# First stage of a hybrid Hyena / FNet / mLSTM block: sums of squares by matmul, one pass for norm and modulation, other load order, two projection blocks accumulated feature by feature

## The chip, the cores and the metric

The kernel runs on one core of a Trainium2 chip. The metric is the device time of one execution in microseconds (us). The engines are called PE (TensorE, with PEld for its weight loads), DVE (VectorE), ACT (ScalarE), POOL (GpSimd) and SP (SyncE, which here only issues DMAs).

## What is computed

One layer over 1024 latent tokens and 256 context tokens of 1024 features. Only the head of it matters here:

```python
mod_l = jnp.split((jax.nn.silu(c) @ ada_w[l] + ada_b[l])[:, None, :], 6, axis=-1)
mod_c = jnp.split((jax.nn.silu(c_ctx) @ ada_w[l] + ada_b[l])[None, None, :], 6, axis=-1)
zc = modulate(rmsnorm(ctx, norm1_w[l]), mod_c[0], mod_c[1]) @ w_in[l] + b_in[l]
zl = modulate(rmsnorm(x, norm1_w[l]), mod_l[0], mod_l[1]) @ w_in[l] + b_in[l]
```

with `rmsnorm(x, w) = x * rsqrt(mean(x*x) + 1e-6) * w` and `modulate(h, shift, scale) = h * (1 + scale) + shift`. Behind it come the three branches, their gated sum, and a mixture of experts.

## The kernel before

Tokens are held transposed: `xs[k]`, k from 0 to 7, is a tile of 128 features by 1024 tokens. PE gets its precision by splitting: a float32 tile becomes `hi` (rounded to fp32r by a copy on ACT) and `lo` (the rest, by a subtraction on DVE; `split`, L213), and `mm3` (L228) issues three fp32r matmuls, hi by hi, hi by lo, lo by hi (L230 to L232). A plain float32 matmul is two MATMUL records in the trace; an fp32r one is one.

`stage_start` (L283) issues the loads on SP's queue in this order: eight of `xs` (512 KB each), the modulation's weights `aw[0..15]` (512 KB each, L321, in `RB` = 6 buffers of tag "r", so the seventh waits until the first is used up), among them the first projection block's weights. Then `ada_first` (L323) runs:

- `norm_in` (L425): eight squares on ACT (L431), added up by seven additions on DVE (L433); eight float32 matmuls with one column (L439) sum over the 128 partitions; square root on ACT (L441, with eps as bias), reciprocal on DVE (L442); a diagonal matrix (L444) and two float32 matmuls (L448) spread r over the partitions into PSUM; eight multiplications on DVE scale `xs` in place (L450).
- four groups g, each for features 2g and 2g+1: eight k-slices of `silu(c) @ ada_w` (L344) into four rows (some in fp32r pieces split beforehand, the others in float32), a copy to SBUF (L347), four small transposes (L350), small additions and a multiplication for shift and scale (L353 to L357), then per feature a `modulate` pass on DVE (L367) and a `split`.

After `ada_first` come `filt_mlp` (L492; two small matmul layers, L501, with a sine between), `ctx_in`, `filt_fold`, and `stage_proj` (L735), whose first loop projects four blocks of `w_fn` (L745): each is 2 halves x 8 features x 3 = 48 matmuls of L230 to L232 into `gp`, followed by blocks of `w_gate`. Tile's scheduler sets the order of each engine's instructions from a list by priority, so work of these functions is interleaved; each engine then runs its list strictly in order.

Of the kernel before, what the change touches and what calls it, by code (L numbers as in the profile page):

```python
# [16 lines left out]
D = 1024  # L17
L = 1024
# [5 lines left out]
EPS = 1e-6  # L24
# [140 lines left out]
class Prog:  # L165
# [22 lines left out]
        self.n += 1  # L188
        return self.dp.tile(list(shape), dt, name=f"{name}_{self.n}", tag=f"{name}_{self.n}")

    PSB = {"gp": 2, "q": 4, "pb": 1, "acc": 6, "ph": 8}

    def ps(self, tag="pb", shape=(128, 1024)):
        self.n += 1
        pool = self.pg if tag == "gp" else self.pp
        return pool.tile(list(shape), F32, name=f"{tag}_{self.n}", tag=tag, bufs=self.PSB[tag])

    def psum(self, name):
# [84 lines left out]
    def stage_start(self):  # L283
        nc = self.nc
        self.pool("T")
        self.pool("TC", "right")
        self.pool("P")
        self.pool("F1", "right")

        self.cs = self.const([128, 8, 4], F32, "cs")  # L290
        nc.gpsimd.memset(self.cs, 0.0)
        cs = self.cs[:, :, 0:2]
        nc.scalar.activation(cs, self.cvec, AF.Silu)
        self.csr = self.const([128, 8, 4], F32R, "csr")
        self.split(self.csr[:, :, 0:2], self.csr[:, :, 2:4], cs)

        nc.scalar.activation(self.const([128, 1], F32, "se"), self.eps, AF.Sqrt)
        self.modc = self.const([128, 48], F32, "modc")
        self.filt_loads()
        self.norm_load()  # L300
        self.ada_loads(0, 12)
        self.w0 = self.load("P", "w", 3, self.A["w_fn"][0], (128, 8, 128))
        self.ada_loads(12, 16)
        self.filt_loads3(0)
        nc.sync.dma_start(self.skip, self.A["skip"])
        self.ada_first()
        self.filt_mlp()
        self.psum("proj")
        self.ctx_in()
        self.filt_fold()  # L310
        self.close("F1")
        self.pool("F2", "right")
        self.filt_spectra()
        self.close("F2")
# [8 lines left out]
    def ada_first(self):  # L323

        nc = self.nc
        ab = self.const([128, 4, 4], F32, "ab")
        for g in range(4):
            nc.vector.tensor_copy(ab[:, g, 0:2], self.ada_b[:, 2 * g:2 * g + 2])
            nc.vector.tensor_scalar(ab[:, g, 2:4], self.ada_b[:, 8 + 2 * g:10 + 2 * g], 1.0, None, op0=ALU.add)
        self.sc, self.sh = self.const([128, 8, 2], F32, "sc"), self.const([128, 8, 2], F32, "sh")  # L330
        self.norm_in()
        self.hT = {"l": []}
        for g in range(4):

            p = self.ps("q", (128, 512))[:4]
            for i in range(4):
                w = self.aw[4 * g + i]
                two = g < 2 and i % 2 == 0
                ws = self.parts("P", "w", 2, w) if two else (w,)
                for j in range(2):  # L340
                    kk = 2 * i + j
                    for x in ws:
                        c = self.csr if two else self.cs
                        nc.tensor.matmul(p, c[:, kk, :], x[:, 512 * j:512 * j + 512], start=kk == 0 and x is ws[0],  # L344
                                         stop=kk == 7)
            row = self.t("F1", "ft", 8, F32, (4, 512))
            nc.scalar.copy(row, p)  # L347
            q = self.ps("q", (128, 4, 4))
            for i in range(4):
                nc.tensor.transpose(q[:, i, :], row[:, 128 * i:128 * i + 128], self.ident[:4, :4])  # L350
            ks = 2 * g, 2 * g + 1
            m = self.t("TC", "m", 2, F32, (128, 4, 2))
            nc.vector.tensor_add(m, q[:, :, 0:2], ab[:, g, :].unsqueeze(2).to_broadcast([128, 4, 2]))  # L353
            nc.vector.tensor_add(m, m, q[:, :, 2:4])
            nc.vector.tensor_copy(self.sh[:, 2 * g:2 * g + 2, :], m[:, 0:2, :])

            nc.vector.tensor_mul(self.sc[:, 2 * g:2 * g + 2, :], m[:, 2:4, :],  # L357
                                 self.n1[:, 2 * g:2 * g + 2].unsqueeze(2).to_broadcast([128, 2, 2]))
            for k in ks:
                t = self.xs[k]  # L360
                self.modulate(t, k, 0)
                hi, lo = self.t("T", "ht", 18, F32R), self.t("T", "ht", 18, F32R)
                self.split(hi, lo, t)
                self.hT["l"].append((hi, lo))

    def modulate(self, t, k, ci):
        self.nc.vector.tensor_scalar(t, t, self.sc[:, k, ci:ci + 1], self.sh[:, k, ci:ci + 1], op0=ALU.mult, op1=ALU.add)  # L367
# [54 lines left out]
    def norm_load(self):  # L422
        self.xs = [self.load("T", "ht", 18, self.A["x_t"][k]) for k in range(8)]

    def norm_in(self):  # L425

        nc = self.nc
        xs = self.xs
        for k in range(8):
            s = self.t("F1", "ft", 8)  # L430
            nc.scalar.activation(s, xs[k], AF.Square)  # L431
            if k:
                nc.vector.tensor_add(acc, acc, s)  # L433
            else:
                acc = s

        p = self.ps("q", (128, 8))
        for t in range(8):
            nc.tensor.matmul(p[:, t:t + 1], acc[:, 128 * t:128 * t + 128], self.ones[:, :1], start=True, stop=True)  # L439
        r = self.const([128, 8], F32, "r")  # L440
        nc.scalar.activation(r, p, AF.Sqrt, bias=self.eps, scale=1.0 / D)  # L441
        nc.vector.reciprocal(r, r)  # L442
        dg = self.t("F1", "ft", 8)
        nc.vector.tensor_mul(dg.rearrange("p (t c) -> p t c", t=8), self.ident.unsqueeze(1).to_broadcast([128, 8, 128]),  # L444
                             r.unsqueeze(2).to_broadcast([128, 8, 128]))
        p = self.ps("pb")
        for a in (0, 512):
            nc.tensor.matmul(p[:, a:a + 512], self.ones, dg[:, a:a + 512], start=True, stop=True)  # L448
        for k in range(8):
            nc.vector.tensor_mul(xs[k], xs[k], p)  # L450


    def filt_loads(self):
# [281 lines left out]
    def stage_proj(self):  # L735
        nc = self.nc
        A = self.A
        bc = self.b_cols
# [2 lines left out]
        self.pool("U")  # L741
        self.yd = self.dram([3, 4, 128, L], name="yd")

        self.fzd = self.dram([4, 128, L], name="fzd")
        for m in range(4):  # L745
            z = self.t("P", "z", 2)
            w = self.wblock(A["w_fn"][m]) if m else self.parts("P", "w", 2, self.w0)
            self.proj_t(w, self.bias_to(z, bc[:, 12 + m:13 + m]))
            nc.sync.dma_start(self.fzd[m], z)

        self.gd = self.dram([3, 8, 128, L], name="gd")
# [14 lines left out]
        for which, n in (("l", L), ("c", LC)):  # L766
            g = self.dram([2, 36, n], name="g" + which)
# [58 lines left out]
        for m in range(8):  # L826
            if m > 1:
                next(tokens)
            w = self.wblock(A["w_qk"][m])
            z = self.t("P", "z", 2)  # L830
# [9 lines left out]
            if m >= 4:  # L840
                z = self.t("U", "zc", 1, F32, (128, LC))
# [12 lines left out]
        for m in range(12):  # L854
            z = self.t("P", "z", 2)
# [1288 lines left out]
```

## Time and profile before

| | |
|---|---|
| three runs, median (lowest to highest) | 1710.73 us (1708.02 to 1713.69) |
| the profiled execution | 1704.3 us |
| its span, first to last instruction | 1702.6 us |
| PE busy in the span | 1572.0 us (92%) |
| DVE busy | 1193.5 us (70%) |
| ACT busy | 679.9 us (40%) |
| POOL busy | 326.4 us (19%) |

The page of the profile gives busy times; the timeline gives each instruction's start and length in us; the windows view gives, for a stretch, each engine's busy time, the granted TensorE clock (PEclk, 1.00 is 2.4 GHz, 0.50 is 1.2 GHz) and the DMA traffic. PEclk comes from records of changes: before the first record it reads 1.00 whatever the clock was.

### The profile page before, as it was taken

What the parts mean: (1) busy time and instruction counts of PE and PEld (TensorE: products, weight loads), DVE (VectorE), ACT (ScalarE), POOL (GpSimd) and SP (SyncE); (2) the same over time, 40 slices, a digit from 0 to 9 for tenths busy, and PEclk for the clock granted to TensorE, in tenths of its full rate; (3) what the DMA queues carried; (4) which work ended last, traced back from release to release, by engine and by line L of the source; (5) the groups of instructions that cost most, each with busy time, mean ns of one, the idle gap of its engine ahead of it and who ended that gap; (6) DMA issues with size and microseconds to landing.
All of it is one profiled execution on the core that took longest, in us unless ns stands there. A gap on an engine that the chain in (4) does not pass through costs nothing. (4 is left out here: it accounts for less than half of the span.)

```text
span 1702.6 us, 22672 instructions
## 1 busy us (share of the span) xinstructions
PE 1572.0 (92%) x8473; PEld 1297.5 (76%) x8473; DVE 1193.5 (70%) x1831; ACT 679.9 (40%) x1029; POOL 326.4 (19%) x288
## 2 busy tenths in 40 slices
PE   3999999999999999899989888899999969999992
PEld 1477777788888887778877777778888869999991
DVE  5678766875876878788645989863255567777766
ACT  4464546423232125444424423232133345544553
POOL 0000000000000001000002200125623353565636
PEclk9999999999999999999999999999999979999996
DMA  7533476522332365976535333585463488999974
GB/s 268 174 128 132 173 251 234 173 78 75 108 117 76 128 233 178 309 272 230 165 111 174 130 100 104 166 311 187 166 225 112 136 251 246 307 281 286 273 216 165
DMA packets 124356, 317.03 MB, mean 186 GB/s; under 512 B 18010, under 2 KB 40530, under 8 KB 124243
## 3 DMA queue, kind: packets, MB, share of 16 engines
q1 hardware_dynamic: 111562, 278.72, 47.8%
q0 software_dynamic: 10496, 32.36, 7.8%
q10 hardware_dynamic: 2184, 4.47, 0.7%
q8 instruction: 68, 1.11, 0.3%
q14 instruction: 46, 0.37, 0.1%
HBM read 226.49 MB, written 89.01 MB: 185 GB/s over the span
## 5 line engine op out<-in xcount | busy, mean ns | idle before, releaser
L230 PE MATMUL gp<-ht,wh 128*128 128x512 f32 x784 | 310.8, 396 | 2.4 <-ACT wh L215 1.3
L232 PE MATMUL gp<-ht,wl 128*128 128x512 f32 x784 | 309.3, 395 | 0.9 <-DVE wl L216 0.9
L231 PE MATMUL gp<-ht,wh 128*128 128x512 f32 x784 | 309.5, 395 | 0.0
L230 PEld LDWEIGHTS gp<-ht,wh 128*128 128x128 f32 x784 | 148.4, 189 | 36.9 <-issue 2.8
L232 PEld LDWEIGHTS gp<-ht,wl 128*128 128x128 f32 x784 | 148.4, 189 | 33.1 <-issue 1.7
L231 PEld LDWEIGHTS gp<-ht,wh 128*128 128x128 f32 x784 | 148.2, 189 | 31.9 <-issue 1.5
L230 PE MATMUL pb<-xh,gh 128*128 128x224 f32 x512 | 142.6, 278 | 0.0
L231 PE MATMUL pb<-xl,gh 128*128 128x224 f32 x512 | 141.5, 276 | 0.0
L232 PE MATMUL pb<-xh,gl 128*128 128x224 f32 x512 | 141.1, 276 | 0.0
L723 DVE SCALAR_TENSOR_TENSOR u<-z,hy_cw,u 128x945 f32<-128x945 f32 (+2 forms) x96 | 117.3, 1222 | 13.5 <-ACT u L715 11.3
L216 DVE TENSOR_TENSOR wl<-w,wh 128x1024 fp32r<-128x1024 f32 x57 | 70.8, 1243 | 65.4 <-ACT wh L215 65.1
L215 ACT CAST wh<-w 128x1024 fp32r<-128x1024 f32 x57 | 59.8, 1048 | 132.0 <-PE gp L231 85.8
L230 PEld LDWEIGHTS pb<-xh,gh 128*128 128x128 f32 x512 | 99.2, 194 | 0.3 <-ACT xh L215 0.2
L231 PEld LDWEIGHTS pb<-xl,gh 128*128 128x128 f32 x512 | 99.2, 194 | 0.1
L232 PEld LDWEIGHTS pb<-xh,gl 128*128 128x128 f32 x512 | 99.1, 194 | 0.0
L723 DVE SCALAR_TENSOR_TENSOR u<-z,ml_cw,u 128x945 f32<-128x945 f32 (+2 forms) x64 | 77.9, 1220 | 26.0 <-ACT u L715 24.9
L708 ACT ACTIVATE z<-gp,b_cols 128x512 f32<-128x512 f32 x48 | 32.9, 685 | 145.4 <-PE gp L232 145.4
L216 POOL TENSOR_TENSOR ml<-m,mh 128x512 fp32r<-128x512 f32 x24 | 35.2, 1467 | 194.0 <-ACT mh L215 189.3
L873 POOL MEMSET z<- 128x1024 f32 x1 | 1.0, 959 | 363.3 <-DVE u L723 363.3
L708 ACT ACTIVATE z<-gp,bh 128x512 f32<-128x512 f32 x46 | 31.5, 686 | 95.0 <-PE gp L232 80.0
L1714 DVE TENSOR_TENSOR gl<-x,gh 128x1024 fp32r<-128x1024 f32 x33 | 40.6, 1232 | 29.4 <-ACT gh L1712 29.4
L1690 POOL DMA_INDIRECT sum<-y,sidx x26 | 42.3, 1626 | 83.3 <-DVE y L1786 80.0
(610 smaller groups left out, 3990.6 us busy)
## 6 DMA issues: line engine op xcount, KB each, us to landing
w<-in_ada_rest SPq DMA_DIRECT2D x32, 512.0 KB
w<-in_w_gu SPq DMA_DIRECT2D x32, 512.0 KB
x<-in_w_gu SPq DMA_DIRECT2D x32, 512.0 KB
w<-in_w_gate SPq DMA_DIRECT2D x24, 512.0 KB
g<-gd SPq DMA_DIRECT2D x24, 512.0 KB
gd<-z SPq DMA_DIRECT2D x23, 512.0 KB
r<-in_ada_in SPq DMA_DIRECT2D x16, 512.0 KB
pd<-ft SPq DMA_DIRECT2D x32, 256.0 KB
```

Source lines behind the costliest of these rows:

```text
L215: self.copied = nc.scalar.copy(hi, src)
L216: return (nc.vector if eng == "v" else nc.gpsimd).tensor_sub(lo, src, hi.bitcast(F32))
L230: mm(ps, lh, rh, start=start, stop=False)
L231: mm(ps, lh, rl, start=False, stop=False)
L232: mm(ps, ll, rh, start=False, stop=stop)
L708: return lambda s, p: self.nc.scalar.activation(z[:, s], p, func, bias=bias, scale=scale)
L723: last = nc.vector.scalar_tensor_tensor(ui[:, r0:r1, c0:c1], zi[:, r0 + dy:r1 + dy, c0 + dx:c1 + dx], taps[:, i:i + 1], ui[:, r0:r1, c0:c1 ...
L873: nc.gpsimd.memset(zt, 0.0)
L1690: return self.nc.gpsimd.indirect_dma_start(out=out, out_offset=bass.IndirectOffsetOnAxis(ap=ix, axis=0), in_=src, in_offset=None, **kw)
L1714: lo = (nc.vector if engines[i] == "v" else nc.gpsimd).tensor_sub(ml, m, mh.bitcast(F32))
```

## The change

- `norm_in` becomes `norm_sums` and `norm_bc`. The additions on DVE are gone: for each of the eight squared tiles, eight float32 matmuls with one column accumulate in PSUM (L461 of the changed kernel), 64 in place of 8; one matmul with the identity puts 1024 eps there first (L456).
- The eight scalings and the eight `modulate` passes become one `scalar_tensor_tensor` per feature, x times scale times r, with r read from PSUM (L361). `hi` is made by an ACT activation that adds the shift (L363), `lo` by a second `scalar_tensor_tensor` (L364).
- The modulation's rows are all plain float32 with two rows of conditioning (L338); no weight of it is split.
- Load order: `aw[0..3]`, `xs[0..7]`, `aw[4..7]`, the weights of projection blocks 0 and 1, `aw[8..15]`.
- PE's order in `ada_first` is the order of the code: rows of group 0, the sums, transposes of group 0, half of group 1's rows, the spreading of r, the other half, then per group the features: as soon as feature k has `hi` and `lo`, its 12 matmuls of blocks 0 and 1 are issued (four PSUM banks: `gp` 2, a new tag `b1` 2, taken from `q`, 4 to 2).
- The silu comes ahead of the square root that loads the table, so that one table load falls away.

```diff
+        self.ada_loads(0, 4)
         self.norm_load()
-        self.ada_loads(0, 12)
-        self.w0 = self.load("P", "w", 3, self.A["w_fn"][0], (128, 8, 128))
-        self.ada_loads(12, 16)
+        self.ada_loads(4, 8)
+        w01 = [self.load("P", "w", 3, self.A["w_fn"][m], (128, 8, 128)) for m in range(2)]
+        self.w01 = [self.parts("P", "w", 2, w) for w in w01]
+        self.ada_loads(8, 16)
...
+        def features(g, r):
+            for k in (2 * g, 2 * g + 1):
+                t, sc, sh = self.xs[k], self.sc[:, k, 0:1], self.sh[:, k, 0:1]
+                nc.vector.scalar_tensor_tensor(t, t, sc, r, op0=ALU.mult, op1=ALU.mult)
                 hi, lo = self.t("T", "ht", 18, F32R), self.t("T", "ht", 18, F32R)
-                self.split(hi, lo, t)
+                nc.scalar.activation(hi, t, AF.Identity, bias=sh)
+                nc.vector.scalar_tensor_tensor(lo, t, sh, hi.bitcast(F32), op0=ALU.add, op1=ALU.subtract)
                 self.hT["l"].append((hi, lo))
+                for (wh, wl), ps in zip(self.w01, blocks):
+                    for q, a in zip(ps, (0, 512)):
+                        self.mm3(q, wh[:, k, :], wl[:, k, :], hi[:, a:a + 512], lo[:, a:a + 512], k == 0, k == 7)
+
+        with self.tc.manual_schedule(engines={mybir.EngineType.PE}):
+            row = rows(0, range(8))
+            r = self.norm_sums()
+            columns(0, row)
+            rows(1, range(4))
+            r = self.norm_bc(r)
+            row = rows(1, range(4, 8))
+            features(0, r)
+            for g in (1, 2, 3):
+                columns(g, row)
+                if g < 3:
+                    row = rows(g + 1, range(8))
+                features(g, r)
...
+        p = self.ps("q", (128, 8))
+        nc.tensor.matmul(p, self.ident, e, start=True, stop=False)
         for k in range(8):
             s = self.t("F1", "ft", 8)
-            nc.scalar.activation(s, xs[k], AF.Square)
-            if k:
-                nc.vector.tensor_add(acc, acc, s)
-            else:
-                acc = s
-
-        p = self.ps("q", (128, 8))
-        for t in range(8):
-            nc.tensor.matmul(p[:, t:t + 1], acc[:, 128 * t:128 * t + 128], self.ones[:, :1], start=True, stop=True)
+            nc.scalar.activation(s, self.xs[k], AF.Square)
+            for t in range(8):
+                nc.tensor.matmul(p[:, t:t + 1], s[:, 128 * t:128 * t + 128], self.ones[:, :1], start=False,
+                                 stop=k == 7 and t == 7)
```

PE's list at its start, before (`q` and `pb` are PSUM tiles, `ft` a squared tile or its sum, `r` one load of modulation weights, `wh`, `wl` split ones):

```order
L439 MATMUL q_212<-ones_80,ft_189 128x1 x8
L344 MATMUL q_237<-wh_238,csr_101 4x512
L344 MATMUL q_237<-wl_239,csr_101 4x512
L344 MATMUL q_237<-wh_238,csr_101 4x512
L344 MATMUL q_237<-wl_239,csr_101 4x512
L344 MATMUL q_237<-r_140,cs_98 4x512
L448 MATMUL pb_226<-ft_224,ones_80 128x512 x2
```

The same place in the changed kernel, up to the first of the projection's matmuls:

```order
L338 MATMUL q_194<-r_124,cs_98 2x512 x2
L456 MATMUL q_207<-deps_205,ident_74 128x8
L461 MATMUL q_207<-ones_80,ft_209 128x1 x8
L461 MATMUL q_207<-ones_80,ft_219 128x1 x8
...
L461 MATMUL q_207<-ones_80,ft_279 128x1 x8
L349 MATMUL q_292<-ident_74,ft_203 128x2 x4
L338 MATMUL q_300<-r_142,cs_98 2x512 x2
L338 MATMUL q_300<-r_144,cs_98 2x512 x2
L476 MATMUL pb_307<-ft_305,ones_80 128x512 x2
L338 MATMUL q_300<-r_146,cs_98 2x512 x2
L338 MATMUL q_300<-r_148,cs_98 2x512 x2
L230 MATMUL gp_188<-ht_317,wh_154 128x512
```

Eight matmuls with one column have become 64, group 0's rows stand ahead of them, and the transposes, half of group 1's rows and the spreading of r stand behind them.

ACT's list of the changed kernel in the middle of the features (`r_179` is the filter's decay load, `r_178` its weights, `ht_423` and `ht_440` are `hi` of features 4 and 5):

```order
L343 COPY ft_367<-q_358 2x512
L554 ACTIVATE r_179<-r_179 128x1024
L552 CAST r_583<-r_178 128x1024
L363 ACTIVATE ht_423<-ht_134,sh_187 128x1024
L363 ACTIVATE ht_440<-ht_136,sh_187 128x1024
L343 COPY ft_420<-q_411 2x512
```

Two instructions of the filter stand ahead of `hi` of feature 4, and each waits for a load that SP issues only when a buffer of tag "r" comes free. On all engines the lists of the two kernels are the same from within `stage_proj` on.

## Rows read from the trace of the kernel before

**Rows 1.** Windows of the span: us, then busy (instructions) by engine, PEclk, DMA, GB/s.

```profile
0.00:57.60 57.60, 30.54 (x80) 8.75 (x80) 35.72 (x50) 24.12 (x27) 1.99 (x10) 0.94 0.77 266
57.60:640.00 582.40, 579.75 (x2520) 457.27 (x2520) 432.14 (x457) 228.09 (x272) 6.02 (x10) 1.00 0.42 146
```

**Rows 2.** Timeline of PE to 42 us: start, length, instructions, idle before and releaser.

```profile
22.29 3.55 PE L439 MATMUL q<-ones,ft 128*128 128x1 f32 x16 [22.29 <-DVE ft L433]
25.70 0.59 PE L344 MATMUL q<-wh,csr 128*4 128x512 f32 x1
26.09 0.63 PE L344 MATMUL q<-wl,csr 128*4 128x512 f32 x1
...
29.06 1.98 PE L448 MATMUL pb<-ft,ones 128*128 128x512 f32 x4
...
31.93 0.39 PE L344 MATMUL q<-wh,csr 128*4 128x512 f32 x1
32.16 0.40 PE L344 MATMUL q<-wl,csr 128*4 128x512 f32 x1
...
35.49 0.41 PE L350 MATMUL q<-ident,ft 4*128 4x4 f32 x4 [0.67 <-ACT ft L347]
35.83 0.39 PE L344 MATMUL q<-wh,csr 128*4 128x512 f32 x1
40.33 1.94 PE L501 MATMUL pb<-ft,fw 33*64 33x512 f32 x2 [4.10 <-issue]
```

**Rows 3.** Timeline of PE from 50 to 83 us.

```profile
50.65 7.03 PE L344 MATMUL q<-r,cs 128*4 128x512 f32 x16
57.61 0.50 PE L230 MATMUL gp<-ht,wh 128*128 128x512 f32 x1
...
80.32 1.98 PE L501 MATMUL pb<-ft,fw 64*128 64x512 f32 x4
82.23 0.50 PE L230 MATMUL gp<-ht,wh 128*128 128x512 f32 x1
```

**Rows 4.** Groups of PE from 57.6 to 80.31 us: busy, mean ns.

```profile
L232 PE MATMUL gp<-ht,wl 128*128 128x512 f32 x21 | 8.3, 397 | 0.0
```

**Rows 5.** A sum of squares late in the filter's folding, timeline of PE.

```profile
153.82 1.84 PE L570 MATMUL pb<-ones,r 128*128 128x1 f32 x16
155.53 0.48 PE L535 MATMUL pb<-r,fh 128*128 128x512 f32 x1
```

**Rows 6.** Windows around two falls of the clock and one rise.

```profile
38.00:40.00 2.00, 0.00 (x0) 0.00 (x0) 2.00 (x2) 0.00 (x0) 0.00 (x0) 0.75 1.09 318
...
44.00:46.00 2.00, 2.00 (x4) 0.26 (x2) 2.00 (x3) 2.00 (x3) 0.00 (x0) 0.54 0.72 211
...
1355.00:1360.00 5.00, 3.96 (x34) 3.73 (x32) 2.39 (x9) 2.47 (x6) 1.26 (x1) 1.00 0.26 105
1360.00:1365.00 5.00, 0.74 (x4) 0.54 (x3) 4.21 (x11) 5.00 (x7) 2.49 (x2) 0.50 0.41 129
```

**Rows 7.** Timeline of PE just ahead of the second fall.

```profile
1357.89 1.05 PE L1583 MATMUL ph<-r_w,hT 128*128 128x20 f32 x8
```

**Rows 8.** The loads' start: one window of 2 us.

```profile
4.00:6.00 2.00, 0.00 (x0) 0.00 (x0) 0.44 (x5) 1.43 (x3) 0.00 (x0) 1.00 0.98 330
```

**Rows 9.** Timeline of ACT: last square, a row copy, the decay's first use.

```profile
18.46 1.06 ACT L431 ACTIVATE ft<-ht 128x1024 f32<-128x1024 f32 x1 [0.98 <-DMA ht<-in_x_t]
...
34.87 0.57 ACT L347 COPY ft<-q 4x512 f32<-4x512 f32 x1 [1.00 <-PE q L344]
...
65.61 1.06 ACT L527 ACTIVATE r<-r 128x1024 f32<-128x1024 f32 x1 [1.26 <-DMA r<-in_decay]
```

**Rows 10.** SP's queue: the decay's load is issued.

```profile
57.71 0.34 SPq L475 DMA_DIRECT2D r<-in_decay  x1
```

**Rows 11.** Groups of DVE to 130 us, the passes over features: busy, mean ns.

```profile
L216 DVE TENSOR_TENSOR ht<-ht,ht 128x1024 fp32r<-128x1024 f32 x8 | 9.4, 1218 | 0.8 <-ACT ht L215 0.8
L450 DVE TENSOR_TENSOR ht<-ht,pb 128x1024 f32<-128x1024 f32 x8 | 9.1, 1216 | 2.3 <-PE pb L448 2.3
...
L367 DVE TENSOR_SCALAR ht<-ht,sc,sh 128x1024 f32<-128x1024 f32 x8 | 6.1, 811 | 0.1
```

More of the change, by code (lines that the diff above doesn't have):

```diff
@@ L189, in dram @@
         return self.dp.tile(list(shape), dt, name=f"{name}_{self.n}", tag=f"{name}_{self.n}")
-    PSB = {"gp": 2, "q": 4, "pb": 1, "acc": 6, "ph": 8}
+    PSB = {"gp": 2, "q": 2, "b1": 2, "pb": 1, "acc": 6, "ph": 8}
     def ps(self, tag="pb", shape=(128, 1024)):
@@ L288, in stage_start @@
         self.pool("F1", "right")
[L290 to L297, printed above, removed]
+        self.cs = self.const([128, 8, 2], F32, "cs")
+        silu = nc.scalar.activation(self.cs, self.cvec, AF.Silu)
+        with self.tc.issue_after(silu.ins):
+            nc.scalar.activation(self.const([128, 1], F32, "se"), self.eps, AF.Sqrt)
         self.modc = self.const([128, 48], F32, "modc")
         self.filt_loads()
+        self.ada_loads(0, 4)
         self.norm_load()
-        self.ada_loads(0, 12)
-        self.w0 = self.load("P", "w", 3, self.A["w_fn"][0], (128, 8, 128))
-        self.ada_loads(12, 16)
+        self.ada_loads(4, 8)
+        w01 = [self.load("P", "w", 3, self.A["w_fn"][m], (128, 8, 128)) for m in range(2)]
+        self.w01 = [self.parts("P", "w", 2, w) for w in w01]
+        self.ada_loads(8, 16)
         self.filt_loads3(0)
@@ L325, in ada_first @@
         nc = self.nc
[L326 to L329, printed above, removed]
+        nb = self.const([128, 8], F32, "nb")
+        nc.vector.scalar_tensor_tensor(nb, self.ada_b[:, 8:16], 1.0, self.n1, op0=ALU.add, op1=ALU.mult)
         self.sc, self.sh = self.const([128, 8, 2], F32, "sc"), self.const([128, 8, 2], F32, "sh")
-        self.norm_in()
@@ L332, in ada_first @@
         self.hT = {"l": []}
-        for g in range(4):
-            p = self.ps("q", (128, 512))[:4]
-            for i in range(4):
[L337 to L361, printed above, removed]
@@ new lines, in ada_first, with rows @@
+        blocks = [[self.ps(tag, (128, 512)) for _ in range(2)] for tag in ("gp", "b1")]
+        def rows(g, ks):
+            if ks[0] == 0:
+                self.rows = self.ps("q", (128, 512))[:2]
+            for kk in ks:
+                nc.tensor.matmul(self.rows, self.cs[:, kk, :], self.aw[4 * g + kk // 2][:, 512 * (kk % 2):512 * (kk % 2) + 512],
+                                 start=kk == 0, stop=kk == 7)
+            if ks[-1] < 7:
+                return
+            row = self.t("F1", "ft", 8, F32, (2, 512))
+            nc.scalar.copy(row, self.rows)
+            return row
@@ new lines, in columns @@
+        def columns(g, row):
+            q = self.ps("q", (128, 4, 2))
+            for i in range(4):
+                nc.tensor.transpose(q[:, i, :], row[:, 128 * i:128 * i + 128], self.ident[:2, :2])
+            s = slice(2 * g, 2 * g + 2)
+            two = lambda a: a[:, s].unsqueeze(2).to_broadcast([128, 2, 2])
+            nc.vector.tensor_add(self.sh[:, s, :], q[:, 0:2, :], two(self.ada_b))
+            sc = self.sc[:, s, :]
+            nc.vector.tensor_mul(sc, q[:, 2:4, :], two(self.n1))
+            nc.vector.tensor_add(sc, sc, two(nb))
@@ L366, in modulate @@
+        self.fzd = self.dram([4, 128, L], name="fzd")
+        for m, ps in enumerate(blocks):
+            z = self.t("P", "z", 2)
+            evac = self.bias_to(z, self.b_cols[:, 12 + m:13 + m])
+            for q, a in zip(ps, (0, 512)):
+                evac(slice(a, a + 512), q)
+            nc.sync.dma_start(self.fzd[m], z)
     def modulate(self, t, k, ci):
@@ L423, in norm_load, with norm_sums, norm_bc @@
         self.xs = [self.load("T", "ht", 18, self.A["x_t"][k]) for k in range(8)]
-    def norm_in(self):
+    def norm_sums(self):
         nc = self.nc
-        xs = self.xs
+        e = self.const([128, 8], F32, "deps")
+        nc.gpsimd.memset(e, D * EPS)
+        p = self.ps("q", (128, 8))
+        nc.tensor.matmul(p, self.ident, e, start=True, stop=False)
         for k in range(8):
             s = self.t("F1", "ft", 8)
-            nc.scalar.activation(s, xs[k], AF.Square)
-            if k:
-                nc.vector.tensor_add(acc, acc, s)
-            else:
-                acc = s
-        p = self.ps("q", (128, 8))
-        for t in range(8):
-            nc.tensor.matmul(p[:, t:t + 1], acc[:, 128 * t:128 * t + 128], self.ones[:, :1], start=True, stop=True)
+            nc.scalar.activation(s, self.xs[k], AF.Square)
+            for t in range(8):
+                nc.tensor.matmul(p[:, t:t + 1], s[:, 128 * t:128 * t + 128], self.ones[:, :1], start=False,
+                                 stop=k == 7 and t == 7)
         r = self.const([128, 8], F32, "r")
-        nc.scalar.activation(r, p, AF.Sqrt, bias=self.eps, scale=1.0 / D)
+        nc.scalar.activation(r, p, AF.Sqrt, scale=1.0 / D)
         nc.vector.reciprocal(r, r)
+        return r
+    def norm_bc(self, r):
+        nc = self.nc
         dg = self.t("F1", "ft", 8)
@@ L448, in norm_in @@
             nc.tensor.matmul(p[:, a:a + 512], self.ones, dg[:, a:a + 512], start=True, stop=True)
-        for k in range(8):
-            nc.vector.tensor_mul(xs[k], xs[k], p)
+        return p
     def filt_loads(self):
@@ L742, in stage_proj @@
         self.yd = self.dram([3, 4, 128, L], name="yd")
-        self.fzd = self.dram([4, 128, L], name="fzd")
-        for m in range(4):
+        for m in range(2, 4):
             z = self.t("P", "z", 2)
-            w = self.wblock(A["w_fn"][m]) if m else self.parts("P", "w", 2, self.w0)
-            self.proj_t(w, self.bias_to(z, bc[:, 12 + m:13 + m]))
+            self.proj_t(self.wblock(A["w_fn"][m]), self.bias_to(z, bc[:, 12 + m:13 + m]))
             nc.sync.dma_start(self.fzd[m], z)
```

## The prediction

> **What bounds the kernel now.** I read the windows view first. From 57.6 to 640 us PE is busy 579.75 of 582.40 us at full clock, and before 57.6 us only 30.54 of 57.60 us [rows 1]. So PE is the limit as soon as it has features to project, and the head is where time can be won. Since PE's list is the same in both kernels from within the projections on, and PE has no slack there, what the head gains or loses should reach the end one for one.
>
> Then the timeline of PE, in order. The first matmul is the sum of squares at 22.29, held by DVE's additions; L344 starts at 25.70; the spreading of r at 29.06 [rows 2]; the first projection matmul at 57.61 [rows 3]. From there PE is dense, with group 2's and 3's rows between. It issues 63 projection matmuls (three groups of 21 [rows 4]) up to the second filter layer, L501 at 80.32, and goes on at 82.23 [rows 3].
>
> That gives the **mark to compare with**. The changed kernel leaves its first stage with 96 projection matmuls (blocks 0 and 1), all modulation rows, r, and the first filter layer done, but not the second. One fp32r matmul of 512 columns takes 0.23 us at full clock (31.93 to 32.16 [rows 2]). Before has 96 of them at 82.23 + 33 x 0.23 = 89.8 us, and without the second layer (1.9 us [rows 3]) that is a mark of **87.9 us**. If the changed kernel finishes its stage at time E, the change is E - 87.9.
>
> **The two clock levels.** The four matmuls from 25.70 start about 0.4 us apart, the same kind at 31.93 and 32.16 0.23 us apart [rows 2]: the first ran at 1.2 GHz, the later at 2.4 (PEclk has no record before the rise). The spreading at 29.06 runs four float32 records of 512 columns in 1.98 us, the pace of L344's sixteen in 7.03 [rows 2, 3], so the rise came within 3.4 us of the first 512-column matmul. After the pause to 40.33, work lasted 5.5 us, to 45.8, before it rose again [rows 2, 6]. And it falls: PE's last matmul before the pause ended at 36.2, and the clock fell at 39.0, 2.8 us later (mean 0.75 in 38 to 40) [rows 2, 6].
>
> What the sums themselves do to it: sixteen records of L439 lasted from 22.29 to 25.7 and the L344 matmuls behind them still ran at half clock [rows 2]. In 1355 to 1360 PE was busy 3.96 of 5 us, at the end with 20-column matmuls [rows 6, 7], and from 1360 the clock was at half. So narrow matmuls, though PE counts as busy, neither raised nor held it in these two places.
>
> **The change, part by part.**
>
> *Sums (the large term).* Eight one-column float32 matmuls cost 22.29 to 25.70 = 3.4 us at 1.2 GHz [rows 2] and 153.82 to 155.53 = 1.7 us at 2.4 GHz [rows 5]. There are now 64: 27 us low, 14 us high, on PE, which waits for r right behind them. The seven additions removed from DVE ended the wait at 22.29, and cost nothing once loads have come.
>
> *Start.* The first load is now `aw[0]`. By 6.0 us the queues had moved 2 us x 330 GB/s = 0.66 MB, more than one load of 0.52 MB [rows 8]: I take 6.2 (an estimate; between 5 and 8). Group 0's eight float32 matmuls cost 0.87 us high (7.03 / 8 [rows 3]) and 1.74 low; with the rise after 4.3 us (between 3.4 and 5.5) that is 2.5 low and 5.5 high: 15.3 us. ACT's list has the row copy (0.57) ahead of the squares (1.06) [rows 9]: the sums start at 17.1. The tokens arrive four loads later, but all eight were squared by 19.5 before [rows 9], and the slow sums leave that cover.
>
> *Sums, dated.* From 15.3 on PE runs nothing wide. I let the clock fall at 19.0, 3.7 us later (bounds: 2.8 as in the pause, and never). Then 1.9 us at the high rate do 1.1 of the eight tiles and the other 6.9 x 3.4 = 23.5 us: **the sums end at 42.5**, where before they ended at 25.7.
>
> *To r.* Transposes 0.4 [rows 2]; four float32 rows and two spreading matmuls are 6 x 0.87 = 5.2 high, 10.4 low. With 4.3 us at the low level they take 7.4, and 0.1 to land: r stands in PSUM at **50.4**. Root, reciprocal and diagonal on ACT and DVE run beside the rows.
>
> *Features.* PE's work: four more rows of group 1 (3.5), groups 2 and 3 (2 x 7.0), 96 x 0.23 = 22.1, three transposes 1.2, the first filter layer 1.9: 42.7 us. DVE needs two passes per feature, 2 x 1.22 = 2.4 us, for 1.22 + 0.81 + 1.22 = 3.2 before [rows 11]; PE needs 12 x 0.23 = 2.8, so PE sets the pace. Two stalls: for `lo` of feature 0 (two L361, one weight split and L364 ahead, 4.8 us after r, where PE's rows end at 3.5): 1.2; and in group 3, where no rows are left to cover transposes, shift, scale, L361 and `hi`: 3.1. Block 2 waits for `gp` to be emptied and its weights split behind the sine's first steps: 1.4. A fall of the clock in the 3.1 us pause: 0.8 (between 0 and 2.5). In all 49.2, so **E = 99.6** and the change is **+11.7 us**.
>
> *Edits at nothing.* The modulation weights' splits leave ACT and DVE, which wait for PE here. One table load less sits under the loads. Two weight blocks ahead of `aw[8]` land well before 42 us. The projection's evacuations move with PE.
>
> *A rule against the trace.* The rows above take the sum's price to follow the clock, 0.21 us a record at one level and 0.11 at the other. The Trainium skill, TensorE: Matmul & The Clock Gate, section LDWEIGHTS, prices a weight load by its columns at 1.2 GHz alone, whatever the level: 107 ns for 128. By it 128 loads would be an estimated 13.7 us at any clock. The 3.4 us of rows 2 speak against it, the 1.7 us of rows 5 agree; it is the third rival below.
>
> **The rivals.**
>
> 1. *The clock stays up through the sums* (not slower). Then they take 14.0 us and end at 31.1; transposes, rows and spreading are 0.4 + 5.2 + 0.1, r at 36.8; 49.2 more give 86.0: -1.9 us. It turns on one thing, whether half the clock is granted while one-column matmuls run. For it: PE has no empty gap there. Against it: rows 2, 6 and 7.
> 2. *ACT is caught behind the decay load.* The filter's L554 and L552 stand ahead of `hi` of feature 4. Before, that load was issued at 57.71 and first used at 65.61, 7.9 us later [rows 9, 10]. Now it is issued when group 2's rows end, 17.4 us after r, so ready at 25.3; with two ACT and two DVE passes behind it, 4.6 us, `lo` of feature 4 is there at 29.9 and PE asks for it at 30.2. A load 3 us later costs 3 us: +15 us.
> 3. *The sums' price does not follow the clock*: 1.7 us for eight at the low level too. They end at 31.1, r at 39.0 since the clock has to rise again, E at 88.2: +0.3 us. Rows 2 speak against it.
>
> **How the numbers follow.** The profiled execution took 1704.3 us, 6.4 under the median of 1710.7. The sum is 1704.3 + 11.7 = 1716.0 against it, and against the median 1722, which I forecast. My own case has 0.62, its range 1715 to 1729 (clock falls and rises 3 us earlier or later each, first load, tail). Rival 1 has 0.13, at 1709; rival 2 0.13, at 1725; rival 3 0.04, at 1711; 0.08 is left for a head that is shorter in some way I do not see. The range 1708 to 1730 takes in all but the last and half the edges. About 0.3%, 5 us, is what a measurement of this kernel can tell from no change. Slower by over that: nearly all of my case and rival 2, 0.72. Within: rivals 1 and 3 mostly and the low edge of mine, 0.16. Faster: 0.12.
>
> **What would show it.** Right: L461's 128 records spread over some 25 us at 0.21 us each, PEclk at 0.50 from about 19 us to some 4 us after they end; r spread at about 50 us; the 96 matmuls done near 98; from then on the same density as before. Wrong: L461 at 0.11 us per record throughout (rival 1 or 3, told apart by PEclk), or r before 40 us. If r comes at 50 and the end does not move, then PE had slack later that I did not see. A pause on `ht` behind L554 is rival 2.

## The result, and the profile after

The changed kernel takes 1742.13 us, the median of four runs (1739.84 to 1744.64); the kernel before took 1711.79 us beside it. The ratio is 1.0178, 95% interval 1.0158 to 1.0198: **slower by 30 us**. Forecast were 1722 us and a range from 1708 to 1730. The direction and the first mechanism came as forecast, the size did not. The profiled execution has a span of 1742.5 us against 1702.6, so 39.9 us are to be found between these two traces. They are more than the 30 us because the profiled execution of the kernel before, 1704.3 us, lies 7.5 us under its median and that of the changed kernel, 1744.2, lies 2.1 us over its own.

The windows view of the changed kernel, as in [rows 1] (us, then busy time and instructions of PE, PEld, DVE, ACT, POOL, PEclk, DMA share, GB/s):

```profile
0.00:104.00 104.00, 91.30 (x313) 54.22 (x314) 30.28 (x40) 28.64 (x32) 1.15 (x10) 0.82 0.49 171
104.00:380.00 276.00, 259.31 (x1062) 195.42 (x1061) 201.03 (x230) 140.64 (x169) 2.00 (x3) 0.97 0.50 174
380.00:640.00 260.00, 260.00 (x1182) 215.24 (x1181) 190.26 (x180) 71.03 (x85) 0.00 (x0) 1.00 0.27 97
```

The head is what the prediction spoke of. The second row is what it did not: between 104 and 380 us PE is idle for 16.7 us, in a stretch where the kernel before was dense [rows 1]. From 380 to 640 us PE is dense again.

Set the two traces beside each other, and the changed kernel is late in two steps. It is 16.5 us late where the first stage ends (104.4 us against the mark of 87.9), and 36.3 us from the matmul that ran at 322 us before; it stays there to 665 us and then drifts to some 40 us at the end. So there are **two losses, 16.5 us and 20 us**. Between them the filter's fold is already 28.9 us late, but PE loses nothing more there: it does other projections first, and has no gap up to 271 us.

**The first loss.** PE's timeline in the head (start, length, instructions, idle before and releaser), to be read beside [rows 2, 3]:

```profile
7.38 9.97 PE L338 MATMUL q<-r,cs 128*2 128x512 f32 x16 [7.38 <-DMA r<-in_ada_in]
17.28 0.39 PE L456 MATMUL q<-deps,ident 128*128 128x8 f32 x2
18.97 26.42 PE L461 MATMUL q<-ones,ft 128*128 128x1 f32 x128 [1.30 <-ACT ft L459]
45.32 0.58 PE L349 MATMUL q<-ident,ft 2*128 2x2 f32 x4
45.84 6.08 PE L338 MATMUL q<-r,cs 128*2 128x512 f32 x8
51.85 1.98 PE L476 MATMUL pb<-ft,ones 128*128 128x512 f32 x4
...
93.59 0.50 PE L230 MATMUL gp<-ht,wh 128*128 128x512 f32 x1 [3.08 <-ACT ht L363]
94.03 2.50 PE L528 MATMUL pb<-ft,fw 33*64 33x512 f32 x4
```

and the windows of its clock (PEclk is the third number from the right):

```profile
18.00:20.00 2.00, 1.03 (x10) 1.03 (x10) 0.00 (x0) 2.00 (x3) 0.00 (x0) 1.00 1.04 414
20.00:22.00 2.00, 2.00 (x12) 2.00 (x12) 0.00 (x0) 2.00 (x3) 0.00 (x0) 0.54 1.01 401
22.00:45.00 23.00, 23.00 (x109) 23.00 (x110) 0.00 (x0) 3.65 (x4) 0.00 (x0) 0.50 0.41 165
...
50.00:52.00 2.00, 2.00 (x5) 0.36 (x4) 0.00 (x0) 0.00 (x0) 0.00 (x0) 0.78 0.76 229
...
96.00:100.00 4.00, 4.00 (x9) 2.81 (x9) 2.19 (x4) 1.20 (x1) 0.00 (x0) 0.50 0.77 255
```

The 128 records of the sums take 26.42 us, 0.21 us each. PE counts as busy in every one of the 23 us from 22 to 45, and all of it is at half clock. The clock falls once more, at 95.2 us, 1.7 us after the 3.08 us pause ahead of the last group: the window from 96 reads 0.50, and the matmuls stand 0.43 us apart there.

**The second loss.** What PE waited for from 104 to 380 us (tile, waiting line, releaser: us in total, times, longest), the five longest in the changed kernel:

```profile
PE pb L230 <- ACT fmh L215: 5.6, 2, 4.1
PE gp L230 <- ACT wvh L215: 3.9, 1, 3.9
PE pb L655 <- DVE kdl L216: 2.9, 1, 2.9
PE pb L230 <- ACT kdh L215: 1.1, 1, 1.1
PE gp L230 <- ACT wh L215: 1.1, 1, 1.1
```

and all there is in the kernel before in the same window:

```profile
PE gp L230 <- ACT wh L215: 1.3, 1, 1.3
PE pb L628 <- DVE kdl L216: 0.7, 1, 0.7
PE gp L231 <- DVE wvl L216: 0.3, 1, 0.3
```

`fm`, `kd` and their halves belong to `filt_spectra`, the last link of the filter's chain (`filt_mlp`, `filt_fold`, `filt_spectra`), whose steps go from PE to ACT, DVE and DMA and back. The wait on `wv` comes at its end: in ACT's list the split of that weight stands behind the last evacuation of the spectra. While a step is on its way, PE does projections. In the changed kernel PE has run out of them before the chain is through.

These waits are not the whole of the 20 us. PE's idle time is 14.4 us more than before (16.6 against 2.3). The rest is clock: it falls three times in the changed kernel between 104 and 380 us, and once in the kernel before (last line):

```profile
187.41:190.82 3.41, 3.41 (x8) 2.41 (x8) 2.54 (x4) 2.10 (x2) 0.00 (x0) 0.50 0.00 0
327.36:334.18 6.82, 5.82 (x14) 4.52 (x15) 2.48 (x3) 0.95 (x2) 0.00 (x0) 0.50 0.14 38
344.42:351.25 6.83, 4.05 (x9) 2.87 (x10) 6.79 (x7) 3.80 (x4) 0.00 (x0) 0.50 0.68 233
...
158.48:161.89 3.41, 3.41 (x8) 2.43 (x8) 1.76 (x3) 0.55 (x1) 0.00 (x0) 0.50 0.32 123
```

PE is busy at half clock for 13.3 us there in place of 3.4, and half of the difference, 5 us, is lost work: 14.4 + 5 is about the 20.

The chain is late because of a buffer. The tile view of `pb`, a PSUM tag with one buffer (counts, min/median/max ns, first and last start):

```profile
L361 DVE SCALAR_TENSOR_TENSOR ht<-ht,sc,pb x8: 1273/1277/1281, 53.9 to 92.2; 128x1024 f32<-128x1024 f32 x8
...
L528 PE MATMUL pb<-ft,fw x8: 589/614/1057, 94.0 to 110.7; 33*64 33x512 f32 x4, 64*128 64x512 f32 x4
```

L361 reads the spread r from `pb` for one feature after the other, the last time at 92.2 us. The filter's two layers use the same tag, so the first starts at 94.0, where it started at 40.3 before [rows 2], and the second at 109.35, where it was 80.32 [rows 3]. In PE's list the fold of the filter now stands behind 166 projection matmuls in place of 113, and starts 28.9 us later (changed kernel, then before):

```profile
124.47 0.58 PE L562 MATMUL pb<-r,fh 128*128 128x512 f32 x1
...
95.56 0.58 PE L535 MATMUL pb<-r,fh 128*128 128x512 f32 x1
```

The last evacuation of the spectra, ACT's L689, starts at

```profile
342.53 0.59 ACT L689 COPY ke<-pb 128x512 f32<-128x512 f32 x1 [2.13 <-PE pb L232]
```

and at 305.11 in the kernel before: 37.4 us, about the delay of what runs behind it (36.3).

### The profile page after: what moved, and what is told of

It is laid out like the page before. It is cut to its first block, busy times and chain, and to the rows that moved or that the text cites. A ratio compares the mean times of both kernels' runs of the same rounds, so it can differ in the third digit from the quotient of the medians.

```text
span 1742.5 us, 22854 instructions
## 1 busy us (share of the span) xinstructions
PE 1611.1 (92%) x8587; PEld 1329.0 (76%) x8587; DVE 1174.2 (67%) x1800; ACT 674.5 (39%) x1023; POOL 326.9 (19%) x288
## 5 line engine op out<-in xcount | busy, mean ns | idle before, releaser
L230 PE MATMUL gp<-ht,wh 128*128 128x512 f32 x768 | 305.4, 398 | 5.8 <-ACT ht L363 3.1
L231 PE MATMUL gp<-ht,wh 128*128 128x512 f32 x768 | 304.1, 396 | 0.9 <-DVE ht L364 0.9
L232 PE MATMUL gp<-ht,wl 128*128 128x512 f32 x768 | 302.6, 394 | 0.9 <-DVE wl L216 0.9
L230 PEld LDWEIGHTS gp<-ht,wh 128*128 128x128 f32 x768 | 145.6, 190 | 42.3 <-issue 4.4
L231 PEld LDWEIGHTS gp<-ht,wh 128*128 128x128 f32 x768 | 145.6, 190 | 33.1 <-DVE ht L364 2.6
L1715 POOL DMA_INDIRECT sum<-y,sidx x26 | 44.8, 1722 | 83.6 <-DVE y L1811 80.5
```

What stands on the lines that cost most here:

```text
L230: mm(ps, lh, rh, start=start, stop=False)
L231: mm(ps, lh, rl, start=False, stop=False)
L232: mm(ps, ll, rh, start=False, stop=stop)
L1715: return self.nc.gpsimd.indirect_dma_start(out=out, out_offset=bass.IndirectOffsetOnAxis(ap=ix, axis=0), in_=src, in_offset=None, **kw)
```

## The experiments

Theory: two losses, the sums on PE at half clock, and the filter's chain held by `pb`. The rival is that the sums alone, or PE's work alone, make the whole loss. All times are medians; the kernel before had 1710.2 to 1712.4 us beside these runs.

The landmarks of the runs, read from their timelines in us: the 96th projection matmul, the start of the first filter layer, the start of the fold, the end of the last evacuation of the spectra, and PE's idle time from 104 to 380 us (gaps over 0.15 us, added up).

| kernel | 96th | layer 1 | fold | spectra end | PE idle | time |
|---|---|---|---|---|---|---|
| before | 89.6 | 40.3 | 95.6 | 305.7 | 2.3 | 1711.8 |
| changed | 104.2 | 94.0 | 124.5 | 343.1 | 16.6 | 1742.1 |
| sums on DVE | 91.3 | 80.0 | 111.6 | 328.3 | 14.8 | 1729.0 |
| r copied | 102.8 | 54.2 | 112.6 | 330.0 | 7.6 | 1733.8 |
| both | 89.4 | 42.6 | 99.2 | 313.7 | 6.1 | 1716.3 |
| before, sums on PE | 100.5 | 52.1 | 106.5 | 316.3 | 1.9 | 1718.0 |

The 96th matmul comes behind the second filter layer (1.9 us) in four of these kernels; in the changed one and in that with the sums on DVE it comes ahead of it, so that these two are 1.9 us later than the column lets them look.

**Sums as before, the rest of the change kept.**

```diff
-            for t in range(8):
-                nc.tensor.matmul(p[:, t:t + 1], s[:, 128 * t:128 * t + 128], self.ones[:, :1], start=False,
-                                 stop=k == 7 and t == 7)
+            if k:
+                nc.vector.tensor_add(acc, acc, s)
+            else:
+                acc = s
+        p = self.ps("q", (128, 8))
+        for t in range(8):
+            nc.tensor.matmul(p[:, t:t + 1], acc[:, 128 * t:128 * t + 128], self.ones[:, :1], start=True, stop=True)
```

> The changed kernel with the sums of squares made as in the kernel before: seven additions on VectorE, eight one-column matmuls. Theory A (two losses: 16.5 us by the end of the first stage, nearly all of it the sums on TensorE at half clock, and some 20 us more up to 360 us because the filter's chain starts later): the sums end near 30.7 us in place of 45.3 and all behind moves up by 14.6 us, to about 1727 us; the second loss stays, since the filter's order is untouched, so it is still some 15 us slower than the kernel before. Theory B (the late sums cause both losses): back to about 1706 to 1712 us. Theory C (the sums are covered by the loads or by VectorE): less than 4 us gained, 1738 us or more.

1729.02 us, ratio 1.0109 (1.0078 to 1.0140): 13 us gained, and still 18 us slower than before. PE's timeline:

```profile
28.05 3.54 PE L462 MATMUL q<-ones,ft 128*128 128x1 f32 x16 [11.89 <-DVE ft L457]
31.52 0.58 PE L349 MATMUL q<-ident,ft 2*128 2x2 f32 x4
```

The sums end at 31.5. They start 5.8 us later than in the kernel before, where they started at 22.29 [rows 2], because four loads of modulation weights now stand ahead of the tokens. The 96th matmul comes at 91.3, 3.6 us later than before once the second filter layer is taken out there, and yet 14.8 us of idle time remain behind it. The first theory holds; the sums are not the whole loss.

**r copied out of `pb`, the rest of the change kept.**

```diff
-        return p
+        b = self.t("F1", "ft", 8)
+        for a in (0, 512):
+            nc.scalar.copy(b[:, a:a + 512], p[:, a:a + 512])
+        return b
```

> The changed kernel, but ScalarE copies the spread r from PSUM to SBUF in two halves and the scalings read it there, so that its PSUM tile is free for the filter's two small layers at once instead of behind the last feature. In TensorE's list the filter's fold then starts behind 130 projection matmuls instead of 166, 36 x 0.23 = 8.2 us earlier. Theory A (the filter's chain, held by that one PSUM tile, sets the end of the stretch up to 360 us): 8 to 11 us gained, less about 1.2 us for the copies ahead of the first scaling: about 1732 us, with TensorE's idle time between 104 and 360 us down from 16.6 us to under 10. Theory B (TensorE's own work and the sums are all there is): within 2 us of 1742, or 1 us slower for the copies.

1733.80 us, ratio 1.0133 (1.0097 to 1.0169): 8.3 us gained with two copies more. PE's waits from 104 to 380 us, the three longest:

```profile
PE gp L230 <- ACT wvh L215: 4.0, 1, 4.0
PE pb L230 <- ACT fmh L215: 1.1, 1, 1.1
PE gp L231 <- DVE wvl L216: 1.1, 1, 1.1
```

The sums still run at half clock and the first stage ends only 3.3 us sooner (1.4 us in the table, and the second layer is done by then), but the fold starts 11.9 us sooner and the spectra end 13.1 us sooner. The waits for `fmh` fall from 5.6 to 1.1 us. So the buffer is a loss of its own. Some of the gain in this trace is not the copy's: group 0's rows took 8.7 us in place of 10.0 and the sums 24.5 in place of 26.4, so r was spread 3 us sooner; and some is lost again, as the clock is at half from 116.4 to 126.7 us, in the fold.

**Both edits.**

> The two edits together: sums as before on VectorE, and r copied out of PSUM. Theory A (two separate losses that add): 14.6 + 8 to 11 us gained, 1717 to 1720 us. Theory B (one loss, the sums): like the first run alone, about 1727 us or where that run came out.

1716.30 us over ten runs, ratio 1.0027 (1.0013 to 1.0041). The spans of the profiled executions fall by 16.1 and 12.9 us for the edits alone and by 27.3 us for both: there they add, to within 2 us. By the medians it is 13.1 and 8.3 us alone and 25.8 for both, so that the copy is worth 8 us by itself and 13 us where the sums are on DVE; on neither reading does one edit make the other needless. What is left of the change (the load order, one pass for norm and modulation, two growing blocks, plain float32 rows) wins nothing here: the 96th matmul stands at 89.4 us, where it stood at 89.6 before, and the fold still starts 3.6 us later.

**Two more gate blocks ahead of the spectra**, as cover for the waiting chain.

```diff
-NG = 8
+NG = 10
```

> The changed kernel with ten gate blocks instead of eight projected ahead of the filter's spectra, work that TensorE has to do anyway and that here stands where it waited for the filter. Theory A (TensorE runs out of other work before the filter's chain is done): 2 x 48 x 0.23 = 22 us more cover, so the 16.6 us of idle time up to 360 us shrink by 10 to 15 us and the time to about 1729 us. Theory B (TensorE is the limit there all through, or the two blocks are missed as cover later on): no change within 3 us.

1760.54 us, ratio 1.0271 (1.0230 to 1.0311): the half about the idle time came, the half about the time did not. PE's longest waits from 104 to 380 us:

```profile
PE pb L230 <- ACT kk L675: 1.4, 1, 1.4
PE pb L655 <- DVE kdl L216: 1.2, 1, 1.2
PE pb L230 <- ACT fmh L215: 0.5, 1, 0.5
```

Idle time there fell from 16.6 to 3.5 us, as it must if PE had lacked work. Behind 640 us it rose from 76.2 to 93.7 us, by 17.5 us: the two blocks had been cover there. That does not yet make the 18.4 us by which this kernel is slower than the changed one, since over the whole span PE's idle time is only some 3 us longer. PE is busy 1627.8 us in place of 1611.1 for the same work, at a mean granted clock of 0.948 in place of 0.959: the rest is half clock, nearly all of it behind 640 us. Theory B's second half ("missed as cover later on") holds, more strongly than written.

**Only the sums, in the kernel before.** The same 64 matmuls in place of the additions, nothing else; an identity times zero clears the PSUM tile.

```diff
-            if k:
-                nc.vector.tensor_add(acc, acc, s)
...
+            for t in range(8):
+                nc.tensor.matmul(p[:, t:t + 1], s[:, 128 * t:128 * t + 128], self.ones[:, :1], start=False,
+                                 stop=k == 7 and t == 7)
```

> The kernel before with only its sums of squares changed: 64 one-column matmuls on TensorE in place of seven additions and eight matmuls (an identity times zero clears the PSUM tile; eps is added where it was). Theory A (the sums run at half clock, 3.4 us for each group, since nothing wide has run yet): they take 27 us from the first square at about 8.5 us on, end near 36 in place of 25.7, and as the filter and the projections both move back by the same 10 us, nothing more is lost behind: about 1721 us. Theory B (the sums hide behind the arrival of the tokens or in the idle time before 57 us): within 4 us of 1711.

1717.96 us, ratio 1.0060 (1.0034 to 1.0086): slower by 8 us in the medians, by 10 in the ratio, where 10 were expected. PE's timeline:

```profile
9.64 27.46 PE L437 MATMUL q<-ones,ft 128*128 128x1 f32 x128 [6.09 <-ACT ft L435]
38.39 0.59 PE L344 MATMUL q<-wh,csr 128*4 128x512 f32 x1 [1.29 <-ACT wh L215]
```

27.46 us as expected; they end at 37.1 in place of 25.7, and everything behind is 10 to 11 us later, the fold too (106.5 against 95.6), without idle time behind it (1.9 us). This is the form that the prediction had in mind: where the filter moves with PE, a late head costs what it is late.

**Wide matmuls among the sums.** Two 512-column float32 matmuls behind each group of sums in the changed kernel, results unused.

```diff
+        wide = self.ps("pb")
...
+            for a in (0, 512):
+                nc.tensor.matmul(wide[:, a:a + 512], self.ones, s[:, a:a + 512], start=True, stop=True)
```

> The changed kernel with two extra float32 matmuls of 512 columns behind each of the eight groups of one-column sums (their result is not used): 16 more matmuls on TensorE. Theory A (one-column matmuls alone let the clock fall, wide ones in between hold it): granted clock 1.00 through the sums, 0.11 us per record, 8 x (1.7 + 0.87) = 20.6 us from 17.2 on, the sums end near 38 in place of 45.3 and the work up to r runs at full clock: r some 10 us earlier, about 1732 us, faster with more work. Theory B (the clock stays at half whatever stands between): 8 x (3.4 + 1.74) = 41 us, the sums end near 58, about 1755 us.

1743.67 us, ratio 1.0185 (1.0159 to 1.0211). PE's timeline, and the window over the sums:

```profile
17.86 1.95 PE L462 MATMUL q<-ones,ft 128*128 128x1 f32 x16 [1.30 <-ACT ft L460]
19.67 1.96 PE L465 MATMUL pb<-ft,ones 128*128 128x512 f32 x4
21.47 1.84 PE L462 MATMUL q<-ones,ft 128*128 128x1 f32 x16
```

```profile
18.00:46.00 28.00, 28.00 (x160) 20.15 (x160) 1.34 (x2) 8.18 (x10) 0.00 (x0) 1.00 0.50 200
```

The clock stays at 1.00 and a group of sums takes 1.70 us, 0.107 us per record, where it took 3.4. My expectation set the two wide matmuls at 0.87 us; that is the price of one ([rows 3]: sixteen records, two per matmul, in 7.03 us), and two take 1.8. So 8 x (1.7 + 1.8) = 28 us fill almost what half clock had cost, and the time is that of the changed kernel with 14 us more work in it. On the clock theory A holds; the gain it promised was my arithmetic.

**Group 1's rows among the sums**, one wide matmul that has to be done anyway behind each group.

```diff
-            r = self.norm_sums()
+            r = self.norm_sums(lambda k: rows(1, [k]))
-            rows(1, range(4))
...
+            self.row1 = more(k)
```

> The changed kernel with the eight matmuls of group 1's modulation rows moved between the eight groups of sums, one 512-column matmul behind each: no work added, nothing left out. Theory A (one wide matmul per group is enough to hold the clock): 8 x (1.7 + 0.44) = 17 us, the sums end near 34.5, r about 15 us earlier, about 1727 us. Theory B (it is not enough, half clock stays): 8 x (3.4 + 0.87) = 34 us, the sums end near 51.5, 3 us later in all, about 1745 us.

1759.66 us, ratio 1.0274 (1.0253 to 1.0296), worse than both numbers. The timeline:

```profile
17.86 1.95 PE L460 MATMUL q<-ones,ft 128*128 128x1 f32 x16 [1.30 <-ACT ft L458]
23.34 1.87 PE L338 MATMUL q<-r,cs 128*2 128x512 f32 x2 [3.54 <-DMA r<-in_ada_in]
25.14 3.58 PE L460 MATMUL q<-ones,ft 128*128 128x1 f32 x16
```

```profile
20.00:22.00 2.00, 0.00 (x0) 0.00 (x0) 0.00 (x0) 2.00 (x3) 0.00 (x0) 0.86 1.03 410
...
24.00:58.00 34.00, 34.00 (x115) 22.50 (x114) 2.36 (x2) 2.94 (x3) 0.00 (x0) 0.50 0.36 132
```

The rows wait for `aw[4]`, which is queued behind the tokens: I had left that load out. In the pause of 3.54 us the clock falls, and from 24 to 58 us it stays at half although a wide matmul stands behind every group. Whether these would have held it without the pause, the run does not tell.

**Trying for a version that beats both.** Three kernels on top of both edits: extra wide matmuls on the squares, in the 12 us in which PE waits for DVE's sums, two for each of seven squares, then one; and, with and without the latter, the transposes of a group moved ahead of the second feature of the group before. The two edits:

```diff
+            if k:
+                nc.tensor.matmul(wide[:, :512], self.ones, s[:, :512], start=True, stop=True)
...
+            features(r, 0)
             for g in (1, 2, 3):
                 columns(g, row)
+                features(r, 2 * g - 1)
                 if g < 3:
                     row = rows(g + 1, range(8))
-                features(g, r)
+                features(r, 2 * g)
+            features(r, 7)
```

> The kernel with both edits (sums on VectorE, r copied), and in TensorE's idle time before the sums two extra 512-column float32 matmuls for each squared tile but the first, paced by the squares (their result is not used): 14 more matmuls. Theory A (they hold the clock through the 12 us of waiting): the sums take 1.7 instead of 3.5 us and the rows behind run at full clock, r 4 to 5 us earlier, about 1711.5 us where the run without them gave 1716.3, level with the kernel before. Theory B (the clock does not follow, or the wait for r is set by VectorE): 1716 to 1718 us.

1719.75 us over twelve runs, ratio 1.0048 (1.0032 to 1.0064). The clock stayed at 1.00 and the sums took 1.84 us, but by the same mistake about the price the fourteen matmuls took 12.25 us and pushed the sums back:

```profile
19.04 12.25 PE L458 MATMUL pb<-ft,ones 128*128 128x512 f32 x28 [2.66 <-ACT ft L456]
31.13 1.84 PE L465 MATMUL q<-ones,ft 128*128 128x1 f32 x16
...
36.86 1.99 PE L479 MATMUL pb<-ft,ones 128*128 128x512 f32 x4
```

> The kernel with both edits (sums on VectorE, r copied) and one extra 512-column float32 matmul, 0.87 us, for each squared tile but the first (the run with two of them pushed the sums back by 2.8 us, so that nothing was won). Theory A (half of TensorE's time with wide matmuls holds the clock, and they fit between the squares): granted clock 1.00 from 19 us on, the sums start at 28.3 and last 1.8 us, r is spread near 34 in place of 37.2: about 1713 us where the run without them gave 1716.3. Theory B (the clock falls all the same, or the gain is lost behind): 1716 to 1718 us.

1715.15 us, ratio 1.0033 (1.0016 to 1.0051): no gain that can be told. Now the matmuls fit, but there is a gap of 1.25 us before the sums, and in these the clock falls:

```profile
28.00:30.00 2.00, 1.40 (x11) 1.40 (x11) 0.55 (x1) 0.00 (x0) 0.00 (x0) 0.90 1.04 414
30.00:32.00 2.00, 2.00 (x11) 1.78 (x12) 0.17 (x3) 0.68 (x2) 0.00 (x0) 0.50 0.71 283
```

> The kernel before this one, with the transposes of each later group moved ahead of the second feature of the group before, so that shift, scale and the first scaling of a group run beside that feature's matmuls. Theory A (the pause ahead of the last group, 2.0 us in the run with both edits, and the half clock behind it go): 4 us more, about 1709 us, level with the kernel before or 2 us faster. Theory B (the pause is the second filter layer's own wait for its sine): no change to the run without it.

> The kernel with both edits and the transposes of each later group moved ahead, without extra matmuls. Theory A: 4 us less than the run with both edits alone (1716.3), about 1712 us. Theory B (the pause is the second filter layer's wait for its sine): 1716 us.

1718.32 us (ratio 1.0041, 1.0024 to 1.0058) and 1720.38 us (1.0046, 1.0027 to 1.0065): both missed. The pause ahead of the last group did not go. In the run without extra matmuls PE's two longest waits in the head behind the sums are

```profile
PE gp L230 <- ACT ht L363: 2.2, 1, 2.2
PE gp L231 <- DVE ht L364: 1.3, 1, 1.3
```

On DVE the last group's first pass now stands behind two steps of the filter's sine (75.4 to 77.8 us) and starts no sooner; on ACT the sine stands behind that group's `hi` (82.8 against 77.8 us), and the second filter layer, which had stood in the pause, slid behind it (88.9 against 78.9 us). No version tried here beats the kernel before.

## Why the prediction was wrong, step by step

*What failed* is the sentence on which the sum was carried to the end: "Since PE's list is the same in both kernels from within the projections on, and PE has no slack there, what the head gains or loses should reach the end one for one." PE had no slack in the kernel before [rows 1] because the filter's chain was early enough. Nor was its list the same at that place: the order of PE's matmuls in the two traces agrees only from the one that ran at 321 us before on, behind the spectra. The mark of 87.9 us counted PE's work at one moment and took out the second filter layer at its price on PE, 1.9 us. But that layer is the start of a chain of 210 us (fold at 95.6, spectra done at 305.7), not a 1.9 us item. In the changed kernel its fold starts 28.9 us later: 16.5 us are the head, and 53 projection matmuls more ahead of it in PE's list at 0.23 us are the other 12.2. The chain then takes 218.6 us in place of 210.1, 8.5 us more. 28.9 + 8.5 = 37.4 us, about what everything behind is late. The run with the copied r had its fold 11.9 us sooner: 36 matmuls fewer ahead of it are 8.3 us, and 3 us of the rest stood already where r was spread. The chain's own matmuls are still 28.9 us late when those of 189 us before run, and 37 at 300: the 8.5 us come in the spectra, where PE waits and the clock falls. Which step of them takes how much was not taken apart.

The list of "edits at nothing" should have held the new reader of r: that L361 reads it from PSUM for as long as the features last is in the diff, and that `pb` has one buffer and serves the filter's layers next is in the code. The prediction even had L528 behind the last group, as 1.9 us of PE work, and did not ask what would wait for it.

*What was right.* The sums: 25.4 us forecast (1.9 at full clock and 23.5 at half), 26.4 measured. The clock's fall was set at 19.0, 3.7 us after group 0's rows, and came at 20.2, 2.9 us after them; its rise was set 4.3 us after the sums and came about 5.5 us after, in the window from 50 to 52. That narrow matmuls neither raise nor hold the clock had thin evidence, 3.4 us in one place [rows 2] and a stretch with gaps in the other [rows 6]; the 26.42 us here, and 27.46 us in the kernel before with the sums on PE, bear it out. *Small misses of the head's terms:* the first load at 7.38 in place of 6.2 (inside 5 to 8), group 0's rows done at 17.3 in place of 15.3 (their sixteen records took 9.97 us where 7.03 is the price at full clock, so some 5.9 us of them ran at half, where 4.3 were set and 5.5 was the bound), so sums ending at 45.3 in place of 42.5 and r spread at 53.8 in place of 50.4. The features took 50.6 us in place of 49.2: the 3.1 us pause came as forecast (3.08), but half clock followed it for some 7 us (95.2 to 102.1), which is 3.4 us of work, over the upper bound of 2.5; the 1.4 us for block 2's wait on `gp` did not come, as PE has no gap from 93.6 to 271 us. E was 104.4 for 99.6. Of the 28.2 us between the sum, 1716.0, and the profiled execution, 1744.2, these are 4.8, the second loss 20, and a drift behind 665 us that no run explains some 3.5. The range, which ended at 1730, had no term for the second loss.

*The rivals.* The clock did not stay up (first rival). L554 did wait for the decay's load, for 4.82 us until 77.00, but no wait of PE followed (second rival). The third, that a record's price does not follow the clock, is settled by two rows: 0.21 us at 0.50 in the changed kernel and 0.107 us at 1.00 where wide matmuls stood between. The Trainium skill, TensorE: Matmul & The Clock Gate, section LDWEIGHTS, gives a weight load as its columns / 1.2, an estimated 107 ns for 128, and names no clock level. The traces agree with it at the full clock alone, and at half clock they read twice that for a load with its one-column matmul.

*What the prediction would have shown.* It named the sign to look for: "If r comes at 50 and the end does not move, then PE had slack later that I did not see." The opposite case, an end that moves by more than the head, was not written down, and it was the one that came. One sign did catch it: "from then on the same density as before" failed, with PE busy 259.3 of 276 us from 104 to 380 where it had been 273.4. The Trainium skill, Perfetto Trace Analysis, section Matmuls, asks that independent groups rotate through different PSUM banks so that the reading of one overlaps the next group; r and the filter's layers, on one tag with one buffer, are a case in which they do not, and the runs with the copied r give its price here, 8 to 13 us.

## What to carry to other kernels

When a change makes a result live longer in PSUM or any shared buffer, list who takes that buffer next and follow that work to the end, not only its own few microseconds: here a 2 us layer that slid by 29 us started a chain of 210 us, and PE ran out of other work to cover it. A dense engine tells that its cover suffices now, not that it will suffice when a side chain starts later. And 26 us of one-column matmuls were paid at half clock here, with PE shown as busy all the while: read the granted clock beside the busy time. Seven additions on an engine that was waiting anyway were the cheaper sum.

## What was not expected of the hardware

- One-column matmuls alone ran 27.46 us from PE's start without a rise of the clock (the kernel before with the sums on PE, 0.21 us a record).
- The granted clock stayed at 1.00 for 28 us while groups of one-column and 512-column matmuls took turns, 1.7 and 1.8 us each; in another run, after a pause of 3.54 us, it stayed at 0.50 for 34 us, with a wide matmul between any two groups.
- In the run with one extra wide matmul per square the clock fell at about 29.6 us, some 2.3 us after the last wide matmul ended, although the sums had been running since 28.6. In the run in which the wide matmuls went on right up to the sums it did not fall.
